# Two heads take turns on TensorE in two attentions; S5's inner product gets 32-column stationary sides in column groups

## The chip, the cores and the metric

The kernel runs on one core of a Trainium2 chip. The metric is the device time of one execution in microseconds (us), the median of several runs. TensorE (PE in the profile) multiplies a stationary operand, loaded by LDWEIGHTS (PEld), with a moving operand that streams through; VectorE is DVE, ScalarE ACT, GpSimd POOL, and SP issues most DMAs.

## The reference

Two model blocks run over 256 tokens of width 2048, one after the other. The parts that the change touches are, in short:

```python
# block 1, sparse attention (NSA): 16 heads of 64, 4 key groups; compressed, selected and window branches
s_c = einsum('bsgrd,bngd->bgrsn', q, kc) * scale + bias_c          # 15 compressed keys
s   = einsum('bqgrd,bqgkd->bgrqk', qc, ks) * scale + bias          # selected; the window branch has the same form
pr  = softmax(s);  o = einsum('bgrqk,bqgkd->bqgrd', pr, vs)
o   = gt[0] * o_c + gt[1] * o_s + gt[2] * o_w
# block 2, layer 0, gated linear attention (GLA): 8 heads, keys of 64
S_t = diag(a_t) S_{t-1} + k_t^T v_t;  o_t = q_t S_t
# block 2, layer 1, S5: 128 groups of 16 channels with 64 complex states, and a skip d
x_t = lam x_{t-1} + b u_t;  y_t = Re(C x_t) + d u_t
```

Around them stand large products with weights (w_in, w_out, MLP, feed forward, gates) in float32 accuracy.

## The kernel before, in words

**The large products.** `group` (L287 on) computes 512 output columns in four tiles of 128. Each weight chunk is loaded by SP, split by ACT (`wh`, L261) and DVE (`wl`, L262) into two fp32r parts, and multiplied by L304. All mixing work is put between these products: a generator (`self.mix`) is advanced one step per weight chunk by `mix_step`, and the S5 preparation (`s5_gen`, `self.bg`) a step or so per group by `bg_step`, at lower priority, so that the scheduler puts its products one by one between those of L304. The order on each engine is fixed when the program is built.

**f32 products.** The mixers multiply in plain f32. The trace records each such product as two MATMUL records (called passes here), each with a LDWEIGHTS of its own. A transpose is one record.

**NSA** (`nsa_gen`, L903 on). A tile t holds two heads, e = 0 on partitions 0 to 63 and e = 1 on 64 to 127. For each unit (t, c, e), c being the half of the 256 queries, `scores` makes two products (L957) of 64 rows by 128 columns into one `px` bank, and a softmax on DVE and ACT (L962 to L971); `turn` transposes (L980) and ACT copies (L982); `values` multiplies by the values (L996, 128 rows by 64 columns, output partitions by e), after L990 for a tile's first unit. One step of the generator does `values` of one unit, `turn` of the next and `scores` of the one after. `comp` (L922) makes the compressed branch's scores, four products of e = 0, then four of e = 1. `px` and `pm` have two banks each.

**GLA** (`gla_gen`, L1255 on). For each of eight levels, `decayed` scales queries and keys two levels ahead (DVE, ACT, POOL), and `scores(lv, e)` makes eight products (L1328, 64 rows by 128 columns; four at the last level, L1335) of one head half e, one e per step; DVE copies them under a mask (L1331). Before it, L1290 makes the diagonal, two banks of one e per step.

**S5's inner matrices** (`prod` and `toep` in `s5_gen`). For each of 16 k, eight products (L1691, stationary 128 by 128, moving 16 columns) give a matrix that ACT copies, POOL adds d to, TensorE transposes (L1699), and ACT copies again; a DMA writes it to DRAM in windows (`TTd`). `s5` later uses products with 32-column stationary sides side by side in four column groups (L1816).

Of the kernel before, what the change touches and what calls it, by code (L numbers as in the profile page):

```python
# [26 lines left out]
# columns of w_in  # L27
# [3 lines left out]
# ------------------------------------------------------------------ host side  # L31
# [26 lines left out]
def layout(inp):  # L58
    """Host side: transposes, reshapes, concatenation and constants of the shapes."""
# [15 lines left out]
    # block-diagonal LRU gates: tile t holds blocks 2t, 2t+1  # L75
# [32 lines left out]
    gm = np.zeros((P, 7, 64), np.uint32)       # gm[s, level, j]: s in the left half of the block of right position j  # L108
# [5 lines left out]
    gp = lambda a: np.ascontiguousarray(a.reshape(64, 2, 64).transpose(1, 2, 0).reshape(P, 64))   # [g, p] -> [(g2 p), pair]  # L114
# [8 lines left out]
    dd = np.zeros((16, 16, 8, 16), np.float32)                                                # [h, k, g, h']  # L123
    dd[np.arange(16), :, :, np.arange(16)] = g["s5_d_2"][0].reshape(16, 8, 16).transpose(2, 0, 1)
    o["s5d"] = dd.reshape(16, 16, P)
# [10 lines left out]
# ------------------------------------------------------------------ device side  # L136
class K:
    def __init__(self, tc, I, out, es, dump=None):
# [16 lines left out]
        self.hold = ()                # instructions the background work stays behind  # L155
# [9 lines left out]
    def bg_step(self, n=1):  # L165
        """emit the next pieces of the work that runs behind the products"""
# [23 lines left out]
    # tiles  # L190
# [62 lines left out]
    def wload(self, pieces, shape=(P, 2, 512)):  # L253
        """pieces: list of (index into tile, dram ap). Returns rounded and rest parts of the chunk."""
# [24 lines left out]
    def mix_until(self, made):  # L279
        """maker of tile k for a product whose operand comes from the mixer, which notes its tiles in made"""  # L280
# [59 lines left out]
    def evac(self, ps, out=None, mul=None, add=None):  # L340
        """out <- (product (+ add)) (* mul), the halves of a wide product added"""
# [26 lines left out]
    # norms  # L368
# [9 lines left out]
    def stat(self, acc, y, k):  # L378
        """acc += y^2 for tile k of 16; the last four stay apart, for TensorE to sum"""
# [8 lines left out]
    def rsqrt_small(self, v, n):  # L388
        """v [128,n] (positive) -> v**-0.5"""
# [14 lines left out]
    def bcast(self, r, dst):  # L404
        """r [128 tok, 2] -> dst [128, 256]: row of r on every partition"""
# [8 lines left out]
    def log_exp(self):  # L414
        """ScalarE's tables for Ln and Exp, after the activation noted last"""
# [10 lines left out]
    def rnorm(self, acc, n, dst, fill=0):  # L426
        """acc [128,256] partial sums of squares -> dst [128,256]: rsqrt(mean+eps) on every partition"""
# [16 lines left out]
        # one Newton step  # L444
# [5 lines left out]
    def rnorm_tok(self, acc, n):  # L450
        """the same with the token on the partition: [128 tok, 2]"""
# [17 lines left out]
    # ------------------------------------------------------------------ stages  # L469
# [30 lines left out]
    def make_x(self, gain):  # L500
        """X <- split(h*gain), a tile at a time: returns X and the maker of tile k"""
# [16 lines left out]
    def post_norm(self, Y, acc, fill=20):  # L518
        """maker of h's tile k: h += Y * rsqrt(mean y^2)   (Y is y times gain)"""
# [15 lines left out]
    def put_ys(self, Y, acc, k0, ys, gain):  # L535
        """Y[k] <- y*gain; acc += y^2"""
# [34 lines left out]
    def exp_small(self, x, n, alloc=None):  # L571
        """exp on [128,n] for -87 < x < 88, to float32 accuracy"""
# [22 lines left out]
    def bias_tables(self):  # L595
        """relative position bias: reversed table in DRAM, and the compressed branch's bias"""
# [12 lines left out]
        # compressed: bias[q, c, e, t, n], distance q + 128c - 16n - 31; the table's column for it is 159 - 128c + 16n,  # L609
        # and past its end every distance is negative  # L610
# [13 lines left out]
    def block1_in(self):  # L624
# [40 lines left out]
        # selected and window keys  # L665
# [9 lines left out]
        # selected and window values, token on the partition  # L675
# [12 lines left out]
        # gates  # L688
# [32 lines left out]
    def thin(self, Xk, wh, wl, n, mul, out=None):  # L721
        """T layout product with few columns, times mul: [n, 256]"""
# [11 lines left out]
    def amode(self, ps, X, c, wh, wl, first, last):  # L734
        """token layout product: ps [128 tok, n] += x[:, chunk c]^T w, w [128 k, n]"""
# [6 lines left out]
    def lru_open(self, UG):  # L742
        V = self.nc.vector
        # c4 = 2*softplus(-lam); halves of the biases
# [747 lines left out]
    def s5_gen(self):  # L1492
# [213 lines left out]
        for k in range(16):  # L1706
# [13 lines left out]
            if pend:  # L1720
                prod()
# [255 lines left out]
```

## Time and profile before

| what | value |
|---|---|
| median of 3 runs | 3699.75 us (3696.19 to 3700.69) |
| span of the profiled execution, first to last instruction | 3695.8 us |
| PE busy | 3534.8 us, 96% |
| DVE, ACT, POOL busy | 63%, 50%, 28% |
| NSA stretch, 206 to 444 us | PE busy 231.3 of 237.6 us |
| GLA stretch, 1405 to 1505 us | PE busy 100.0 of 100.0 us |
| mean granted TensorE clock | 0.981 |

The profiled execution's own time beside its span is not listed; the runs lie 0.4 to 4.9 us above the span. A record's duration on PE overlaps the next record's, so what a product costs is read from the distance between starts: how much later the products behind it start than at their usual pace.

### The profile page before, as it was taken

To read this page: it belongs to the slowest core of one execution; us is meant where nothing else is said; L and a number is where in the kernel's file an instruction comes from. 1 tells how busy PE (TensorE), PEld (TensorE's weight loads), DVE (VectorE), ACT (ScalarE), POOL (GpSimd) and SP (SyncE) were. 2 spreads that over 40 slices of the span, in tenths; PEclk is the share of its full clock that TensorE was granted. 3 is DMA by queue.
4 is the path that set the end of the run, shared out by engine and by line. 5 is a ranking of instruction groups with operands and counts; after the bars stand their busy time and mean duration, and the time that the engine had idled before them with its cause. 6 is when DMAs were issued, how large, how long until landed. Compare 5 with 4: busy or idle time off the path is not lost. (4 is left out here: it accounts for less than half of the span.)

```text
span 3695.8 us, 59166 instructions
## 1 busy us (share of the span) xinstructions
PE 3534.8 (96%) x22214; PEld 3113.5 (84%) x22214; DVE 2337.9 (63%) x3610; ACT 1836.0 (50%) x2895; POOL 1020.8 (28%) x1466
## 2 busy tenths in 40 slices
PE   8989989999999999999899999999779999999998
PEld 8878878888888898999887888888668888888887
DVE  6676596566656775455865466666765765565556
ACT  4655564544445653445544344444555554444444
POOL 1221122288730112011615555555410200000000
PEclk9999999999999999999999999999989999999999
DMA  8644345666776564565567777777776466565663
GB/s 214 204 117 139 115 144 190 187 199 204 231 219 195 175 201 123 143 177 181 164 197 218 224 215 229 235 220 258 251 228 186 145 189 187 185 191 188 188 188 128
DMA packets 506552, 699.61 MB, mean 189 GB/s; under 512 B 43239, under 2 KB 317671, under 8 KB 506264
## 3 DMA queue, kind: packets, MB, share of 16 engines
q1 hardware_dynamic: 472848, 628.60, 54.9%
q0 software_dynamic: 27120, 63.05, 5.9%
q10 hardware_dynamic: 6296, 4.17, 0.4%
q8 instruction: 174, 2.85, 0.3%
q14 instruction: 114, 0.93, 0.1%
HBM read 654.22 MB, written 37.22 MB: 187 GB/s over the span
## 5 line engine op out<-in xcount | busy, mean ns | idle before, releaser
L304 PE MATMUL ps<-x,wh 128*128 128x512 f32 (+1 forms) x8560 | 2503.9, 355 | 68.3 <-ACT wh L261 21.3
L262 DVE TENSOR_TENSOR wl<-wr,wh 128x1024 fp32r<-128x1024 f32 x1126 | 1432.1, 1277 | 1132.6 <-ACT wh L261 1123.3
L304 PE MATMUL ps<-x,wl 128*128 128x256 f32 x6832 | 1924.2, 283 | 1.3 <-DVE wl L262 1.3
L261 ACT ACTIVATE wh<-wr 128x1024 fp32r<-128x1024 f32 x1126 | 1184.7, 1057 | 1311.4 <-PE ps L304 1023.9
L304 PEld LDWEIGHTS ps<-x,wh 128*128 128x128 f32 x8560 | 1511.2, 191 | 321.8 <-ACT wh L261 22.9
L304 PEld LDWEIGHTS ps<-x,wl 128*128 128x128 f32 x6832 | 1305.5, 191 | 10.8 <-issue 3.5
L304 PE MATMUL px<-x,wh 128*128 128x512 f32 (+1 forms) x1776 | 660.1, 397 | 12.5 <-DVE x L249 7.0
L304 PE MATMUL px<-x,wl 128*128 128x256 f32 x1744 | 492.4, 282 | 1.2 <-DVE wl L262 1.2
L304 PEld LDWEIGHTS px<-x,wh 128*128 128x128 f32 x1776 | 333.8, 189 | 91.1 <-DVE x L249 8.5
L304 PEld LDWEIGHTS px<-x,wl 128*128 128x128 f32 x1744 | 331.6, 190 | 2.7 <-DVE wl L262 2.1
L527 POOL TENSOR_TENSOR e<-x,r_c 128x256 f32<-128x256 f32 x40 | 34.6, 871 | 1039.3 <-DVE r_c L448 1026.9
L1748 POOL TENSOR_TENSOR m<-m,m 128x256 f32<-128x256 f32 x64 | 64.5, 1020 | 326.8 <-PE pm L1691 236.8
L357 ACT ACTIVATE e<-ps 128x256 f32<-128x256 f32 x324 | 119.9, 376 | 67.6 <-PE ps L304 57.9
L376 POOL TENSOR_TENSOR acc<-acc,sq 128x256 f32<-128x256 f32 x89 | 79.6, 894 | 260.4 <-ACT sq L375 257.8
L245 ACT ACTIVATE x<-e 128x256 fp32r<-128x256 f32 x168 | 67.9, 410 | 88.6 <-DVE e L1473 42.8
L246 DVE TENSOR_TENSOR x<-e,x 128x256 fp32r<-128x256 f32 x168 | 78.0, 473 | 27.7 <-ACT x L245 25.1
L1731 POOL TENSOR_TENSOR m<-m,m 128x128 f32<-128x128 f32 x128 | 86.0, 694 | 10.7 <-DMA TTd<-m 10.7
L361 DVE TENSOR_TENSOR e<-ps,e 128x256 f32<-128x256 f32 x168 | 69.8, 416 | 6.3 <-ACT e L357 6.3
L1730 POOL TENSOR_TENSOR m<-m,m 128x128 f32<-128x128 f32 x128 | 70.1, 575 | 0.3
L1749 POOL TENSOR_TENSOR m<-m,m 128x256 f32<-128x256 f32 x64 | 64.1, 1002 | 5.3 <-DMA BBd<-m 1.8
L738 PE MATMUL ps<-wh,x 128*128 128x512 f32 x160 | 64.7, 405 | 0.0
L1750 POOL TENSOR_TENSOR m<-m,m 128x256 f32<-128x256 f32 x64 | 62.4, 974 | 2.1
(495 smaller groups left out, 2977.8 us busy)
## 6 DMA issues: line engine op xcount, KB each, us to landing
wr<-in_w_ffn_in_dram SPq DMA_DIRECT2D x704, 256.0 KB, 3.3
wr<-in_mlp_w_dram SPq DMA_DIRECT2D x256, 512.0 KB, 4.3
wr<-in_w_ffn_out_dram SPq DMA_DIRECT2D x176, 512.0 KB, 4.3
wr<-in_w_in_dram SPq DMA_DIRECT2D x152, 512.0 KB, 3.8
wr<-in_w_out_dram SPq DMA_DIRECT2D x64, 512.0 KB, 3.7
wr<-in_w_glu_dram SPq DMA_DIRECT2D x128, 256.0 KB, 3.2
wr<-in_ple_gate_dram SPq DMA_DIRECT2D x32, 512.0 KB, 4.5
wr<-in_w_in_dram SPq DMA_DIRECT2D x32, 256.0 KB, 5.4
```

The lines of the kernel that those rows point to most:

```text
L245: a = nc.scalar.activation(dst[:, 0], src, AF.Copy)
L246: b = (eng or nc.vector).tensor_tensor(dst[:, 1], src, dst[:, 0].bitcast(F32), op=ALU.subtract)
L261: nc.scalar.activation(wh, wr, AF.Copy)
L262: nc.vector.tensor_tensor(wl, wr, wh.bitcast(F32), op=ALU.subtract)
L304: mm = lambda o, w, x, a, z: nc.tensor.matmul(o, w, x, start=a, stop=z, skip_group_check=True)
L357: a = S.activation(t, ps[:, T:2 * T], AF.Copy)
L361: self.hold = a, V.tensor_tensor(y, ps[:, 0:T], t, op=ALU.add)
L376: (eng or nc.vector).tensor_tensor(acc, acc, q, op=ALU.add)
L738: nc.tensor.matmul(ps, xh, wh, start=first, stop=False, skip_group_check=True)
L1730: G_.tensor_tensor(cx[:, q], u_(0), l_(0), op=ALU.mult)
L1731: G_.tensor_tensor(t1[:, q], u_(1), l_(1), op=ALU.mult)
L1748: G_.tensor_tensor(ob[:, :, ri], v4(gb[0][:, 0]), v4(gb[1][:, ri]), op=ALU.mult)
```

## The change

In NSA the unit is now (t, c). `products` makes the score products of both heads, e = 0 and 1 in turn, into two `px` banks; `soft` does one head's softmax, one per step; the transposes of e = 0 and e = 1 come in the two following steps, and `values` takes both heads, in turn, another step later. `comp` alternates e as well. In GLA both e of a level are multiplied in one step, alternating, into two banks; the masked copies of e = 0 come in that step and those of e = 1 in the next. In S5 the operands of the inner product change sides: the stationary side is B for two groups of channels side by side with zeros in the other's place (32 columns), the moving side C (128 columns), the output a quarter of the partitions; two products add up in it. Its result needs no transpose, d comes as [128, 16], and one ACT copy, one PE transpose and one `pm` tile go per k.

```diff
 # nsa_gen
-            for e in range(2):
-                ps = self.ps("px")
-                for t in range(4):
-                    nc.tensor.matmul(ps[:, t * 16:t * 16 + 15], q[e * 64:e * 64 + 64, th * 4 + t, c * P:(c + 1) * P],
+            pss = [self.ps("px") for _ in range(2)]
+            for t in range(4):
+                for e in range(2):
+                    nc.tensor.matmul(pss[e][:, t * 16:t * 16 + 15], q[e * 64:e * 64 + 64, th * 4 + t, c * P:(c + 1) * P],
...
+        def products(u):
+            t, c = u
...
+            ps = [self.ps("px") for _ in range(2)]
+            for b in range(2):
+                for e in range(2):
+                    er = slice(e * 64, e * 64 + 64)
+                    nc.tensor.matmul(ps[e][:, b * T:b * T + nk], q[er, t, c * P:(c + 1) * P], ksw[b][er, t // 2, 0:nk],
+                                     start=True, stop=True)
+            return ps
+        def soft(u, e, ps):
...
-                nc.tensor.matmul(yp[e * 64:e * 64 + 64, c * P:(c + 1) * P], vv[b][:, kc, g * 64:g * 64 + 64], PT[:, i],
-                                 start=False, stop=(i == n - 1), skip_group_check=True)
+                for e in range(2):
+                    nc.tensor.matmul(yp[e * 64:e * 64 + 64, c * P:(c + 1) * P], vv[b][:, kc, g * 64:g * 64 + 64],
+                                     PT[e][:, i], start=False, stop=(i == n - 1), skip_group_check=True)
...
-            for u in [(t, c, e) for t in range(th * 4, th * 4 + 4) for c in range(2) for e in range(2)]:
+            for u in [(t, c) for t in range(th * 4, th * 4 + 4) for c in range(2)]:
                 if u2:
                     values(*u2)
-                u2 = (u1[0], turn(*u1)) if u1 else None
-                u1 = (u, scores(u))
+                PT = [turn(u1[0], u1[1][0])] if u1 else None
+                ps = products(u)
+                pr = [soft(u, 0, ps[0])]
+                yield 1
+                if u1:
+                    PT.append(turn(u1[0], u1[1][1]))
+                    u2 = u1[0], PT
+                pr.append(soft(u, 1, ps[1]))
+                u1 = u, pr
                 yield 1
 # gla_gen
-            for e in range(2):
-                yield 1
-                scores(lv, e)
+            yield 1
+            pss = scores(lv)
+            keep(lv, 0, pss[0])
+            yield 1
+            keep(lv, 1, pss[1])
 # s5_gen, prod and toep
-            for q in range(8):
-                nc.tensor.matmul(kt[:, q * 16:q * 16 + 16], cx[q // 4][:, q % 4].rearrange("p t h -> p (t h)"),
-                                 bb[:, q], start=True, stop=True)
-            S.activation(bt[:, 2], kt[:, 0:P], AF.Copy)
-            G_.tensor_tensor(bt[0:16, 2], bt[0:16, 2], bt[0:16, 3], op=ALU.add)
...
-            nc.tensor.transpose(pt[:, 0:P], bt[:, 2], self.ident)
+            for i in range(2):
+                for r in range(4):
+                    q = 2 * r + i
+                    nc.tensor.matmul(kt[r * 32:r * 32 + 32, 0:P], bt[:, i, r * 32:r * 32 + 32],
+                                     cx[q // 4][:, q % 4].rearrange("p t h -> p (t h)"), start=(i == 0), stop=(i == 1),
+                                     skip_group_check=True)
...
+            G_.tensor_tensor(kp[:, 112:128], kp[:, 112:128], bt[:, 2, 0:16], op=ALU.add)
...
-            G_.tensor_tensor(bb, cb[:, 1, 0], n_(0), op=ALU.mult)
-            G_.tensor_tensor(t1, cb[:, 1, 1], n_(1), op=ALU.mult)
-            G_.tensor_tensor(bb, bb, t1, op=ALU.add)
+            for w in range(2):
+                G_.tensor_tensor(cb[:, 1, w], cb[:, 1, w], n_(w), op=ALU.mult)
+            for i in range(2):
+                G_.tensor_tensor(bt[:, i].rearrange("p (r two) h -> p r two h", two=2, h=16)[:, :, i],
+                                 pairs(cb[:, 1, 0])[:, :, i], pairs(cb[:, 1, 1])[:, :, i], op=ALU.add)
```

On PE, in the first half of NSA, before the change (`pm` 2853 is the output of tile t = 2, `px` 2916 its scores):

```order
L304 MATMUL ps_2821<-x_86,wh_2933 128x256
L980 MATMUL pm_2797<-cst,m_2749 128x128
L990 MATMUL pm_2853<-x_721,VB 128x256
L980 MATMUL pm_2797<-cst,m_2749 128x128
L304 MATMUL ps_2821<-x_86,wh_2933 128x256
L304 MATMUL ps_2821<-x_86,wl_2934 128x256
L304 MATMUL ps_2822<-x_86,wh_2933 128x256 x2
L996 MATMUL pm_2853<-m_2800,x_721 64x128 x2
L957 MATMUL px_2916<-x_720,q 128x256 x2
L304 MATMUL ps_2822<-x_86,wl_2934 128x256
```

The same engine and half after the change (L999 is the former L990, L1006 L996, L988 L980, L960 L957):

```order
L304 MATMUL ps_2356<-x_87,wl_2692 128x256
L999 MATMUL pm_2719<-x_721,VB 128x256
L1006 MATMUL pm_2719<-m_2622,x_721 64x128
L1006 MATMUL pm_2719<-m_2675,x_721 64x128
L1006 MATMUL pm_2719<-m_2622,x_721 64x128
L1006 MATMUL pm_2719<-m_2675,x_721 64x128
L988 MATMUL pm_2725<-cst,m_2630 128x128 x4
L960 MATMUL px_2735<-x_720,q 128x128
L960 MATMUL px_2736<-x_720,q 128x128
L960 MATMUL px_2735<-x_720,q 128x128
L960 MATMUL px_2736<-x_720,q 128x128
L304 MATMUL ps_2355<-x_87,wh_2755 128x256 x2
```

Both heads' values and scores now stand in one piece at a chunk's boundary, alternating; 14 of the 16 score units stand like this, the other two (t = 0, c = 0 and t = 3, c = 1) still have L304's between their heads.

On PE, the first of S5's inner products (k = 0), before:

```order
L304 MATMUL px_10255<-x_9275,wl_10372 128x256
L1691 MATMUL pm_10232<-m_9318,m_9537 128x16
L304 MATMUL px_10256<-x_9275,wh_10371 128x512
L1691 MATMUL pm_10232<-m_9318,m_9537 128x16
L304 MATMUL px_10256<-x_9275,wl_10372 128x256
```

The same after (L1720 is the former L1691):

```order
L1720 MATMUL pm_10236<-m_9539,m_9318 32x128
L304 MATMUL px_10261<-x_9275,wh_10376 128x512
L1720 MATMUL pm_10236<-m_9539,m_9318 32x128
L304 MATMUL px_10261<-x_9275,wl_10377 128x256
L1720 MATMUL pm_10236<-m_9763,m_9318 32x128
L304 MATMUL ps_10262<-x_9275,wh_10376 128x512
```

The products stand where they stood: over all 16 k, before, 88 alone between L304's, eight fours and one eight; after, 88 alone, eight fours, a three and a five. The rest of the order on PE is as before, apart from the 16 transposes of L1699 that are gone.

## Rows read from the trace of the kernel before

**Rows 1.** Page, part 1: busy us (share of the span) xinstructions, by engine.
```profile
PE 3534.8 (96%) x22214; PEld 3113.5 (84%) x22214; DVE 2337.9 (63%) x3610; ACT 1836.0 (50%) x2895; POOL 1020.8 (28%) x1466
```

**Rows 2.** Windows NSA and GLA: length, busy us by engine (x instructions), clock, DMA.
```profile
206.40:444.00 237.60, 231.27 (x1620) 201.25 (x1619) 144.20 (x458) 124.74 (x281) 30.53 (x39) 0.97 0.39 121
1405.00:1505.00 100.00, 100.00 (x627) 86.06 (x626) 58.47 (x160) 38.54 (x45) 27.95 (x16) 1.00 0.40 116
```

**Rows 3.** Timeline, PE, two NSA score units: start us, us, engine, line, xpasses.
```profile
255.44 1.13 PE L957 MATMUL px<-x,q 64*128 64x256 f32 x4
...
265.32 0.28 PE L304 MATMUL ps<-x,wh 128*128 128x256 f32 x1
265.53 0.71 PE L957 MATMUL px<-x,q 64*128 64x128 f32 x4
266.17 0.39 PE L304 MATMUL ps<-x,wh 128*128 128x256 f32 x1
266.39 0.28 PE L304 MATMUL ps<-x,wl 128*128 128x256 f32 x1
```

**Rows 4.** Timeline, PE, values of one head at c = 1.
```profile
420.44 0.28 PE L304 MATMUL ps<-x,wh 128*128 128x256 f32 x1
420.70 1.09 PE L996 MATMUL pm<-m,x 128*64 128x128 f32 x8
421.72 0.39 PE L304 MATMUL ps<-x,wh 128*128 128x256 f32 x1
421.94 0.28 PE L304 MATMUL ps<-x,wl 128*128 128x256 f32 x1
422.06 0.40 PE L304 MATMUL ps<-x,wh 128*128 128x256 f32 x2
```

**Rows 5.** Timeline, PE, GLA's scores of one e at level 0.
```profile
1429.34 2.00 PE L1328 MATMUL px<-x 64*128 64x64 f32 x16
1431.26 0.50 PE L738 MATMUL ps<-wh,x 128*128 128x512 f32 x1
1431.60 0.39 PE L739 MATMUL ps<-wl,x 128*128 128x512 f32 x1
1431.83 0.40 PE L740 MATMUL ps<-wh,x 128*128 128x512 f32 x1
```

**Rows 6.** Timeline, PE: compressed scores of both e, of one, and S5's column groups.
```profile
206.59 1.53 PE L922 MATMUL px<-kcmp,q 64*128 64x15 f32 x16
...
328.63 1.06 PE L922 MATMUL px<-kcmp,q 64*128 64x15 f32 x8
...
2705.42 0.64 PE L1816 MATMUL px<-wh,x 128*32 128x128 f32 x16
```

**Rows 7.** Timeline, PE, one of S5's inner products between L304's.
```profile
974.53 0.28 PE L304 MATMUL px<-x,wl 128*128 128x256 f32 x1
974.64 0.29 PE L1691 MATMUL pm<-m,m 128*128 128x16 f32 x2
974.79 0.48 PE L304 MATMUL px<-x,wh 128*128 128x512 f32 x1
975.10 0.29 PE L1691 MATMUL pm<-m,m 128*128 128x16 f32 x2
```

**Rows 8.** Timeline, PE, a lone f32 product of a narrow tile between L304's.
```profile
56.91 0.28 PE L304 MATMUL ps<-x,wl 128*128 128x256 f32 x1
57.12 1.03 PE L603 MATMUL px<-oh,relb 33*16 33x511 f32 x2
58.07 0.50 PE L304 MATMUL ps<-x,wh 128*128 128x256 f32 x2
58.41 0.28 PE L304 MATMUL ps<-x,wl 128*128 128x256 f32 x1
```

**Rows 9.** Waits of PE in the NSA window: us in total, times, longest us.
```profile
PE pm L942 <- DVE m L936: 4.0, 1, 4.0
PE pm L980 <- DVE m L971: 2.0, 4, 1.3
```

More of the change, by code (lines that the diff above doesn't have):

```diff
@@ L945, in nsa_gen @@
         Bts, yps = {}, {}
-        def scores(u):
-            t, c, e = u
-            if c == 0 and e == 0:
+        def products(u):
+            t, c = u
+            if c == 0:
                 Bts[t] = Bt = self.m([P, 2, T])
-                for e_ in range(2):
-                    nc.gpsimd.dma_start(Bt[:, e_], tab[2 * t + e_])
-            Bt, nk, off, hh = Bts[t], P * (c + 1), P * (1 - c), 2 * t + e
-            er = slice(e * 64, e * 64 + 64)
-            ps = self.ps("px")
-            for b in range(2):
-                nc.tensor.matmul(ps[:, b * T:b * T + nk], q[er, t, c * P:(c + 1) * P], ksw[b][er, t // 2, 0:nk],
-                                 start=True, stop=True)
+                for e in range(2):
+                    nc.gpsimd.dma_start(Bt[:, e], tab[2 * t + e])
+            nk = P * (c + 1)
+            ps = [self.ps("px") for _ in range(2)]
[6 more added lines that the diff above has]
+        def soft(u, e, ps):
+            t, c = u
+            Bt, nk, off, hh = Bts[t], P * (c + 1), P * (1 - c), 2 * t + e
             pr = self.m([P, 2, T])
@@ L985, in values @@
         def values(u, PT):
-            t, c, e = u
+            t, c = u
             g, r2 = t // 2, (t % 2) * 64
-            if c == 0 and e == 0:
+            if c == 0:
                 yps[t] = self.ps("pm")
@@ L995, in values @@
                 b, kc = i // (c + 1), i % (c + 1)
-                nc.tensor.matmul(yp[e * 64:e * 64 + 64, c * P:(c + 1) * P], vv[b][:, kc, g * 64:g * 64 + 64], PT[:, i],
-                                 start=False, stop=(i == n - 1), skip_group_check=True)
-            if c == 1 and e == 1:
+                for e in range(2):
+                    nc.tensor.matmul(yp[e * 64:e * 64 + 64, c * P:(c + 1) * P], vv[b][:, kc, g * 64:g * 64 + 64],
+                                     PT[e][:, i], start=False, stop=(i == n - 1), skip_group_check=True)
+            if c == 1:
                 y = yp[:, 0:T]
@@ L1284, in gla_gen @@
         EQ = [yv[:, 3072:4096].rearrange("p (i t) -> p i t", i=4), gl[:, 12:16]]
-        for e in range(2):
-            er = slice(e * 64, e * 64 + 64)
-            for b in range(2):
-                ps = self.ps()
-                for i in range(4):
-                    nc.tensor.matmul(ps[:, i * P:(i + 1) * P], gk[er, i, b * P:(b + 1) * P], gq[er, i, b * P:(b + 1) * P],
-                                     start=True, stop=True)
-                V.tensor_tensor(ST[:, e, b], ps.rearrange("p (i t) -> p i t", i=4),
+        for b in range(2):
+            pss = [self.ps() for _ in range(2)]
+            for i in range(4):
+                for e in range(2):
+                    er = slice(e * 64, e * 64 + 64)
+                    nc.tensor.matmul(pss[e][:, i * P:(i + 1) * P], gk[er, i, b * P:(b + 1) * P],
+                                     gq[er, i, b * P:(b + 1) * P], start=True, stop=True)
+            for e in range(2):
+                V.tensor_tensor(ST[:, e, b], pss[e].rearrange("p (i t) -> p i t", i=4),
                                 self.ident[:, None, :].to_broadcast([P, 4, P]), op=ALU.mult)
@@ L1316, in decayed, with scores, keep @@
             G.tensor_tensor(eb[:, :, 0], blk(gk)[:, :, 0], eb[:, :, 0], op=ALU.mult)
-        def scores(lv, e):
+        def scores(lv):
             half = 1 << lv
             qk = EQ[lv % 2]
-            er = slice(e * 64, e * 64 + 64)
-            ps = self.ps()
-            if lv < 7:
-                for b in range(2):
-                    for i in range(4):
-                        right = qk[er, i, b * P:(b + 1) * P].rearrange("p (n two h) -> p n two h", two=2, h=half)[:, :, 1]
-                        o = (b * 4 + i) * 64
-                        nc.tensor.matmul(ps[:, o:o + 64], qk[er, i, b * P:(b + 1) * P], right, start=True, stop=True)
+            pss = [self.ps() for _ in range(2)]
+            for m in range(8 if lv < 7 else 4):
+                b, i = m // 4, m % 4
+                for e in range(2):
+                    er = slice(e * 64, e * 64 + 64)
+                    if lv < 7:
+                        right = qk[er, i, b * P:(b + 1) * P].rearrange("p (n two h) -> p n two h", two=2, h=half)[:, :, 1]
+                        o, left = pss[e][:, m * 64:m * 64 + 64], qk[er, i, b * P:(b + 1) * P]
+                    else:
+                        o, left, right = pss[e][:, i * P:(i + 1) * P], qk[er, i, 0:P], qk[er, i, P:T]
+                    nc.tensor.matmul(o, left, right, start=True, stop=True)
+            return pss
+        def keep(lv, e, ps):
+            half = 1 << lv
+            if lv < 7:
                 dst = ST[:, e].rearrange("p b i t -> p (b i) t").rearrange("p m (n two h) -> p m n two h", two=2, h=half)
@@ L1333, in scores @@
             else:
-                for i in range(4):
-                    nc.tensor.matmul(ps[:, i * P:(i + 1) * P], qk[er, i, 0:P], qk[er, i, P:T], start=True, stop=True)
                 S.activation(ST2[:, e], ps.rearrange("p (i t) -> p i t", i=4), AF.Copy)
@@ L1342, in gla_gen @@
                 decayed(lv + 1)
-            for e in range(2):
-                yield 1
-                scores(lv, e)
+            yield 1
[3 more added lines that the diff above has]
+            keep(lv, 1, pss[1])
         while "vr" not in self.ready:
@@ L1708, in s5_gen @@
             cb, ll = self.m([P, 2, 2, 8, 16]), self.m([P, 2, 8, 8])
-            bt = self.m([P, 4, P])
+            bt = self.m([P, 3, P])
+            G_.memset(bt[:, 0:2], 0.0)
             src = I["s5cb"][k]
@@ L1712, in s5_gen @@
             G_.dma_start(ll, LD[:, :, kg:kg + 8])
-            G_.dma_start(bt[0:16, 3], I["s5d"][:, k])
-            bb, t1 = bt[:, 0].rearrange("p (g h) -> p g h", g=8), bt[:, 1].rearrange("p (g h) -> p g h", g=8)
+            G_.dma_start(bt[:, 2, 0:16], I["s5d"][:, k])
             n_ = lambda w: self.rp[:, w, kg:kg + 8].unsqueeze(2).to_broadcast([P, 8, 16])
-            G_.tensor_tensor(bb, cb[:, 1, 0], n_(0), op=ALU.mult)
-            G_.tensor_tensor(t1, cb[:, 1, 1], n_(1), op=ALU.mult)
-            G_.tensor_tensor(bb, bb, t1, op=ALU.add)
+            pairs = lambda a: a.rearrange("p (r two) h -> p r two h", two=2)
+            for w in range(2):
+                G_.tensor_tensor(cb[:, 1, w], cb[:, 1, w], n_(w), op=ALU.mult)
+            for i in range(2):
+                G_.tensor_tensor(bt[:, i].rearrange("p (r two h) -> p r two h", two=2, h=16)[:, :, i],
+                                 pairs(cb[:, 1, 0])[:, :, i], pairs(cb[:, 1, 1])[:, :, i], op=ALU.add)
             yield 1
             if pend:
-                prod()
+                kp = prod()
             cxs = []
@@ L1754, in s5_gen @@
                 yield 1
-                prod()
+                kp = prod()
                 yield 1
-                toep()
+                toep(kp)
                 pend = None
```

22 lines of the change are left out of this document (11 added, 11 removed).

## The prediction

> **What bounds the kernel now.** I read the page's busy shares first, then the windows of the stretches that the change touches, then PE's timeline inside them, and the waits last. PE is busy for 96% of the span [rows 1], and in the stretches themselves for 231.3 of 237.6 us (NSA) and 100.0 of 100.0 us (GLA), while DVE is busy for 144.2 and 58.5 us of them and ACT for 124.7 and 38.5 [rows 2]. So time that goes on PE there is time that goes from the span, as long as the softmax and the weight splitting keep up; they have room for about a third more work in the same time.
>
> Busy time on PE says little of what a product costs, since records overlap. The reader is to look at distances between starts. L304's narrow products start every 0.12 us (421.94 to 422.06) [rows 4]. Two passes of a score product of 64 rows are put in between: from 265.32 to 266.39 pass 1.07 us, of which two L304's usual 0.24, so the four passes of a unit at c = 0 cost 0.83 [rows 3]. Passes of 128 columns follow each other every 0.11 (the eight of rows 4 take 1.09 against a first one of some 0.3), so 4 x 0.11 = 0.44 are passes and 0.39 is the price of going in and out: the next L304 comes 0.64 after the first pass instead of 0.44, the one behind it 0.22 later instead of 0.12, and the first pass 0.21 after the last L304 [rows 3]. A block costs 0.39 plus its passes. At c = 1 the four passes last 0.42 longer (1.13 against 0.71), so a unit costs 1.25 [rows 3]. Eight passes of values: 420.44 to 421.94 less 0.24 is 1.26; four, then, 1.26 - 0.44 = 0.82 [rows 4]. Sixteen passes of GLA: 1429.34 to 1431.60 less one L738 of 0.23 (1431.60 to 1431.83), plus 0.09 on the way in as in rows 3, is 2.12 [rows 5].
>
> Do two halves of the array run beside each other? Compressed scores of one head half (8 passes) last 1.06, of e = 0 and then e = 1 in one block (16) 1.53 and not 1.06 + 0.88 = 1.94 [rows 6]: the second half's rows started while the first's passes were still queued. And 16 passes in four column groups last 0.64 [rows 6] where 16 in one group last 2.00 [rows 5]. So both row groups and column groups overlap here; alternated, two equal streams should take the time of one.
>
> **The change part by part.**
>
> Scores of NSA. Now 16 units at 0.83 and 16 at 1.25: 33.3 us. After: by the order 14 pairs stand together and cost one unit each, 7 x 0.83 + 7 x 1.25 = 14.6, and two pairs stay apart (2 x 0.83 + 2 x 1.25 = 4.2): 18.8. Gain 14.5.
>
> Values. Now 16 x 0.82 + 16 x 1.26 = 33.3; after, half of it, since the two heads' outputs lie in different column groups, and column groups run beside each other in S5's products [rows 6]. Gain 16.6. The Trainium skill, "TensorE: Matmul & The Clock Gate", section "The mechanism", speaks against it: by it a weight load overlaps a running product only where the row group differs, which column groups do not. By that rule two column streams would follow each other, and the gain would be 6.2 (rival 2); the 16 passes in 0.64 us [rows 6] do not agree with it.
>
> Compressed scores. Now four blocks of 8 passes (0.39 + 0.88 = 1.27) and two of 16, 0.47 longer (1.53 - 1.06): 1.74; together 8.6. After, four blocks of 16 passes in two streams, 1.27 each: 5.1. Gain 3.5.
>
> Waits in NSA. PE waits 4.0 us for L936 and 2.0 for L971 [rows 9]. The first belongs to the compressed softmax, whose DVE work is the same: it stays. The second goes, since a transposition comes two steps after its scores instead of one. Gain 2. What is late next: `products` takes both `px` banks, and the one of e = 1 is read by DVE only a step (some 24 L304's, 2.9 us) before it is wanted again. The reads stand at the head of that step's DVE work, so I cost this at nothing; if DVE were late, L304 behind it would wait and with it everything (the third rival). The softmax results and their transposes are held longer in the nine 2 KB tiles; four are taken per unit and are free again by the next unit but one: nothing.
>
> GLA. Now 14 blocks of 2.12, two of 16 passes on the diagonal, some 2.15 each, and two of 8 at the last level, 1.27: 36.5. After, 7 x 2.12, two blocks of 8 beside 8 (1.27) and one of 4 products beside 4 (1.27): 18.7. Gain 17.8. Behind it DVE has 16 masked copies per level instead of two times 8, the same work; `decayed` still has its three steps until its scores. Cost nothing; cover: DVE's 58 of 100 us become 58 of 82.
>
> S5. Here the products stay one by one between L304's. Now one costs 0.23: from 974.64 to 975.10 pass 0.46, of which one wide L304 0.23 [rows 7]. 88 of these are 20.2, eight fours at no more than 4 x 0.23 and an eight make some 9, and 16 transposes of a pass each 1.8: 31. After, each has a tile of 32 columns. The trace has one product of this kind alone between L304's: 56.91 to 58.41 is 1.50, less three L304's 0.36 is 1.14, less its two passes of 511 columns leaves 0.28 for going in and out [rows 8]: 128 more columns cost a pass 0.105 (rows 3, 0.42 over four passes), so one of 511 takes 0.11 + 3 x 0.105 = 0.43. I take 0.30. With two passes of 128 columns: 0.30 + 0.22 = 0.52. 98 blocks (88 alone, ten groups, whose column groups overlap) make 98 x 0.52 = 51. Loss 20. Bounds: as now, 0.23, if the way in and out cost nothing more (then 22.5 and a gain of 8), and 0.61, if it cost the 0.39 of rows 3 (60, a loss of 29). I take 0.52, the row with the nearest shape.
>
> The rest of S5 is off PE: POOL has one memset and one small addition more and one product less per k, ACT one copy less; POOL is at 28% [rows 1], and nothing on PE waits for it there. The skip's DMA has 128 short rows instead of 16 long ones, 16 times, on POOL's queue behind the same loads: nothing.
>
> Sum: 14.5 + 16.6 + 3.5 + 2 + 17.8 = 54.4 gained, 20 lost: 34. The span of 3695.8 becomes 3661.5; the runs' median lies 4 us above the span, so 3699.75 - 34 = 3665.5, call it 3665.
>
> **The rivals.**
>
> 1. S5's products cost what they cost now. For it: they are surrounded by L304's today too and pay 0.23. Against it: today's tile is the whole array like L304's, and the lone narrow product pays more [rows 8]. Gain 8 instead of loss 20: 3637.
>
> 2. Column groups do not gain from alternating. The overlap part of the values' gain is lost and only the ways in and out are saved, 16 x 0.39 = 6.2 instead of 16.6: 3676. For it: a weight load of one group has to pass the other group's running product, and the trace has no two alternating column groups of 64. Against it: four groups of 32 take 0.64 us for 16 passes [rows 6]. It is what the page named at the values would give.
>
> 3. NSA becomes bound by something else. Its 238 us shrink to about 201 and DVE's 144 stay: 72%, with each softmax a chain through DVE, ACT and DVE and only two `px` banks. If half of NSA's 36.6 comes back as waits: 3683.
>
> 4. Slower than before: each of a lone S5 product's two passes pays the way in and out by itself, because the second pass's weights cannot be loaded while the array changes its tile. Price 2 x 0.52 = 1.04 per product, 102 us instead of 31, a loss of 71 against 54: 3716. It decides from 85 / 98 = 0.87 us per product. Against it: in rows 8 both passes together paid 0.3.
>
> 5. The change does not do what it says: alternated row and column groups run one after the other, since each product's two passes hold up the next. Then only the ways in and out go: 14 for scores, 16 for values and 8 for GLA at 0.39 are 15 us, with the waits 17, against 20: 3703. Against it: rows 6, as far as they show a block of one half behind a block of the other.
>
> **How the numbers follow.** The forecast 0.60, with a range of its own of 3652 to 3678 (S5 at 0.61 and at 0.40); rival 1 0.10, rival 2 0.08, rival 3 0.11, rival 4 0.07, rival 5 0.04. The range 3636 to 3686 takes in the forecast and rivals 1 to 3. A difference of 0.2% (7.4 us) is about what a measurement can tell from none: faster than that are the forecast and rivals 1 to 3, 0.89; within it rival 5, 0.04; slower rival 4, 0.07.
>
> **What would show it.** In the profile of the changed kernel: L960's eight passes in about the 0.71 and 1.13 us that four take now; L1006's 16 in about 1.1; L1350's 32 in about 2.0, and GLA's stretch some 18 us shorter. Between L304's, L1720's two passes with starts 0.5 us further apart than L304's pace, and S5's stretches longer by about 20 us in all. Wrong would be: L304's of NSA with waits on DVE or ACT beyond the 6 us of now; a pair in two times 0.71; L1720 at 0.23 or beyond 0.87.

## The result, and the profile after

| | median us | lowest to highest |
|---|---|---|
| before | 3699.26 | 3696.19 to 3700.69 |
| after | 3661.01 | 3654.79 to 3666.71 |

The ratio is 0.9896 (95% interval 0.9876 to 0.9916): 38 us faster, forecast 34. The span went from 3695.8 to 3655.6 us, 40.2 less. By first starts of the same lines, NSA with what follows it up to the first L424 took 33.8 us less (236.4 instead of 270.2), GLA 18.0 less (113.5 instead of 131.4), and the two stretches with S5's products 7.7 more (436.9 instead of 429.2) and 4.4 more (951.7 instead of 947.2); the rest is under 2 us a piece.

Page, part 1, and the windows of NSA and GLA, which answer to [rows 1, 2]:

```profile
PE 3501.3 (96%) x22198; PEld 3060.9 (84%) x22198; DVE 2353.4 (64%) x3610; ACT 1833.1 (50%) x2879; POOL 1022.5 (28%) x1498
```

```profile
206.40:410.30 203.90, 195.80 (x1599) 176.96 (x1599) 142.91 (x463) 124.40 (x285) 29.75 (x41) 0.96 0.45 139
1377.40:1459.40 82.00, 82.00 (x628) 70.72 (x627) 59.90 (x160) 38.52 (x45) 27.02 (x16) 1.00 0.49 141
```

DVE and ACT do in the shorter stretches what they did in the longer ones: DVE 142.91 us where it had 144.20, now 70% of the time. Softmax and masked copies kept up.

The timeline of PE (start us, us, engine, line, shapes, passes): compressed scores of both heads, values of both at c = 1, a pair of scores at c = 0 and one at c = 1 [rows 3, 4, 6]:

```profile
206.56 1.07 PE L922 MATMUL px<-kcmp,q 64*128 64x15 f32 x16
...
246.43 1.09 PE L1006 MATMUL pm<-m,x 128*64 128x128 f32 x16
...
256.85 0.72 PE L960 MATMUL px<-x,q 64*128 64x128 f32 x8
...
265.26 1.13 PE L960 MATMUL px<-x,q 64*128 64x256 f32 x8
```

Eight passes of scores take the 0.71 and 1.13 us that four took, sixteen of values the 1.09 of eight; compressed scores fall from 1.53 to 1.07. Of GLA's level the reader sees the two streams themselves:

```profile
1399.81 0.32 PE L1350 MATMUL px<-x 64*128 64x64 f32 x1
1399.98 0.27 PE L1350 MATMUL px<-x 64*128 64x64 f32 x1
1399.98 0.27 PE L1350 MATMUL pm<-x 64*128 64x64 f32 x1
1400.09 0.27 PE L1350 MATMUL px<-x 64*128 64x64 f32 x1
...
1401.75 0.50 PE L738 MATMUL ps<-wh,x 128*128 128x512 f32 x1
```

`px` and `pm`, the two heads, start within 0.01 us of each other, and behind the first pair one comes every 0.11 us. The whole level lasts from 1399.81 to 1401.75, 1.94 us: 32 passes in the time that 16 took, 1429.34 to 1431.26 [rows 5].

S5's lone product [rows 7]:

```profile
1035.70 0.50 PE L304 MATMUL px<-x,wh 128*128 128x512 f32 x1
1036.13 0.41 PE L1720 MATMUL pm<-m,m 128*32 128x128 f32 x2
1036.47 0.38 PE L304 MATMUL px<-x,wl 128*128 128x256 f32 x1
1036.78 0.41 PE L1720 MATMUL pm<-m,m 128*32 128x128 f32 x2
```

From 1036.13 to 1036.78 pass 0.65 us, of which a narrow L304 is 0.12: 0.53 where it was 0.23.

Waits of PE in the NSA window [rows 9]:

```profile
PE pm L943 <- DVE m L937: 4.5, 1, 4.5
PE px L436 <- POOL acc L376: 2.3, 1, 2.3
...
PE pm L988 <- DVE m L979: 0.3, 1, 0.3
```

The compressed softmax still stops PE (4.5), the transposes nearly no more (0.3 instead of 2.0), and there is a new wait: L436, which sums squares for a norm of another part, comes 17.5 us earlier than before (293.0 instead of 310.5) and now waits 2.3 us for POOL's additions. Behind this wait the granted clock was 0.50 (1.2 GHz) from 293.8 to 304.0 us, and four score passes of 256 columns took 1.95 us instead of 1.13:

```profile
293.63 1.95 PE L960 MATMUL px<-x,q 64*128 64x256 f32 x4
```

### The profile page after: what moved, and what is told of

Same layout as the page of the kernel before. It is cut to its first block, busy times and chain, and to the rows that moved or that the text cites. A ratio compares the mean times of both kernels' runs of the same rounds, so it can differ in the third digit from the quotient of the medians.

```text
span 3655.6 us, 59158 instructions
## 1 busy us (share of the span) xinstructions
PE 3501.3 (96%) x22198; PEld 3060.9 (84%) x22198; DVE 2353.4 (64%) x3610; ACT 1833.1 (50%) x2879; POOL 1022.5 (28%) x1498
## 5 line engine op out<-in xcount | busy, mean ns | idle before, releaser
L304 PE MATMUL ps<-x,wh 128*128 128x512 f32 (+1 forms) x8560 | 2498.4, 355 | 62.1 <-DVE e L361 19.3
L304 PE MATMUL ps<-x,wl 128*128 128x256 f32 x6832 | 1922.4, 283 | 0.8 <-DVE wl L262 0.8
L304 PEld LDWEIGHTS ps<-x,wh 128*128 128x128 f32 x8560 | 1510.7, 191 | 319.5 <-issue 30.3
L304 PEld LDWEIGHTS ps<-x,wl 128*128 128x128 f32 x6832 | 1306.1, 191 | 11.1 <-issue 5.6
L304 PE MATMUL px<-x,wh 128*128 128x512 f32 (+1 forms) x1776 | 658.3, 396 | 11.2 <-DVE x L249 6.8
L304 PE MATMUL px<-x,wl 128*128 128x256 f32 x1744 | 491.7, 282 | 0.5 <-DVE wl L262 0.5
L304 PEld LDWEIGHTS px<-x,wh 128*128 128x128 f32 x1776 | 332.6, 189 | 94.4 <-DVE x L249 8.6
L304 PEld LDWEIGHTS px<-x,wl 128*128 128x128 f32 x1744 | 330.5, 190 | 4.8 <-issue 3.2
L246 DVE TENSOR_TENSOR x<-e,x 128x256 fp32r<-128x256 f32 x168 | 86.0, 521 | 26.4 <-ACT x L245 22.6
L1779 POOL TENSOR_TENSOR m<-m,m 128x256 f32<-128x256 f32 x64 | 59.6, 932 | 71.7 <-DMA m<-in_s5bT_dram 71.0
L1780 POOL TENSOR_TENSOR m<-m,m 128x256 f32<-128x256 f32 x64 | 73.7, 1152 | 0.1
L738 PE MATMUL ps<-wh,x 128*128 128x512 f32 x160 | 64.6, 404 | 0.0
L740 PE MATMUL ps<-wh,x 128*128 128x512 f32 x160 | 63.2, 395 | 0.0
```

The lines of the kernel that those rows point to most:

```text
L246: b = (eng or nc.vector).tensor_tensor(dst[:, 1], src, dst[:, 0].bitcast(F32), op=ALU.subtract)
L304: mm = lambda o, w, x, a, z: nc.tensor.matmul(o, w, x, start=a, stop=z, skip_group_check=True)
L738: nc.tensor.matmul(ps, xh, wh, start=first, stop=False, skip_group_check=True)
L1780: G_.tensor_tensor(t1, v4(gb[0][:, 1]), v4(gb[1][:, 1 - ri]), op=ALU.mult)
```

## The experiments

All were timed beside the kernel before; its median was 3689 to 3699 in these sets, so kernels of different sets are compared by their ratios to it. A "price by starts" is summed over all pieces of a line: how much later the products behind a piece start than at L304's usual pace.

**Attentions alone (e1_attn) and S5 alone (e2_s5).** The layout of d and `s5_gen` from `prod` on are exchanged between the two kernels; e1_attn, against the changed kernel:

```diff
-                    nc.tensor.matmul(kt[r * 32:r * 32 + 32, 0:P], bt[:, i, r * 32:r * 32 + 32],
-                                     cx[q // 4][:, q % 4].rearrange("p t h -> p (t h)"), start=(i == 0), stop=(i == 1),
+                nc.tensor.matmul(kt[:, q * 16:q * 16 + 16], cx[q // 4][:, q % 4].rearrange("p t h -> p (t h)"),
+                                 bb[:, q], start=True, stop=True)
```

> The changed kernel with S5's inner product as it was before (stationary 128 by 128, moving 16 columns, one transpose per k); both attentions alternate. By starts on TensorE, the S5 products of the changed kernel cost 54.3 us (98 blocks) and those of before 33.5 (with the transposes). Theory A, each lone product with a 32-column tile costs the program its 0.53 us instead of 0.23: 3661 - 20.7 = 3640. Rival B, part of that time is taken out of waits that stand in the same stretch (from the first S5 product to the S5 layer's first rows the changed kernel lost only 7.7 + 4.4 = 12.1 us): 3649. Rival C, the S5 part costs nothing in all: 3661.

> The kernel before with the S5 part of the change alone. Theory A (0.53 us instead of 0.23 for a lone product, and the transposes gone): 3699 + 20.7 = 3720. Rival B (part of it comes out of waits of the same stretch): 3699 + 12 = 3711. Rival C (S5 costs nothing): 3699. In the profile the lone products of L1720's form should again cost 0.53 by starts.

Measured: attentions alone 3636.27, ratio 0.9853 (0.9832 to 0.9875): a gain of 54 us. S5 alone 3716.91, ratio 1.0073 (1.0051 to 1.0094): a loss of 27. By starts S5's products cost 32.0 (e1_attn, with the transposes) and 54.6 us (e2_s5, 98 places). C is out. The changed kernel once more, beside the same runs of before, is to tell A from B:

> The changed kernel once more, beside the runs of the kernel before on the chip of these experiments, so that it is compared with the others there. Ratio to before as in the first measurement, 0.9896 (0.9876 to 0.9916). With before at 3689 as in the first four experiments that is 3651; the S5 part would then have cost 15 (attentions alone, 3636) to 28 us (S5 alone, 3717 against 3689), the 20 of the forecast between them.

3654.51, ratio 0.9887 (0.9864 to 0.9911). From e1_attn's 0.9853 to the two ratios of the changed kernel it is 13 to 16 us, from before to e2_s5 27; A's 21 lies between, B's 12 is not excluded.

**One after the other in a piece (e4_serial), and longer turns (e5_turns).** The loops over e go outside the products, or half outside:

```diff
-            for m in range(8 if lv < 7 else 4):
-                b, i = m // 4, m % 4
-                for e in range(2):
+            for e in range(2):                      # e4; scores, values, comp and the diagonal alike
+                for m in range(8 if lv < 7 else 4):
+                    b, i = m // 4, m % 4
```

> The changed kernel, with the same products in the same pieces, but in a piece first all of e = 0, then all of e = 1 (scores, values, compressed scores of NSA, all of GLA's scores). Theory A, only taking turns lets two halves of the array run beside each other: a piece grows by half its passes at 0.11 (0.21 where they have 256 columns): scores 7 x 0.44 + 7 x 0.86 = 9.1, values 8 x 0.44 + 8 x 0.88 = 10.6, compressed scores 4 x 0.47 = 1.9, GLA 7 x 1.76 + 2 x 0.88 + 0.88 = 15: 36.6 in all, 3698. Rival E, a piece of one half behind a piece of the other overlaps too, as the compressed scores did in the kernel before (16 passes in 1.53 us instead of 1.94): a half of that, 3679. Rival F, the gain was the ways in and out alone: 3661, unchanged.

> The changed kernel with longer turns: scores, values, compressed scores and GLA's diagonal change the head every two products (four passes), GLA's levels every four products (eight passes). Theory G, which the pieces of one half behind the other suggest (scores, 4 passes behind 4: 1.36 against 1.29 us, nothing lost; values, 8 behind 8: 1.77 against 1.28; GLA, 16 behind 16: 3.67 against 2.13): the passes of one half run beside the last three or four of the other. Then turns of four passes cost what turns of two do (values at c = 1 1.28, compressed scores 1.19, diagonal 1.29 a piece), and GLA's levels, with three changes, lie at 2.8 to 3.2 us: 7 us slower than the changed kernel. Rival H, only turns of a single product overlap: values 1.77, compressed scores 1.66, diagonal 1.84, GLA 3.67: 17 us slower.

e4_serial: 3672.27, ratio 0.9958 (0.9941 to 0.9975), against 0.9896 and 0.9887: some 25 us lost. By starts a level of GLA costs 3.67 us instead of 2.13, values of both heads at c = 1 1.77 instead of 1.28, compressed scores 1.66 instead of 1.19; pairs of scores lose next to nothing. All pieces together lose 18 us. A's 37 and F's nothing are both wrong, E's half is close, and the timeline of PE shows why:

```profile
1407.47 1.66 PE L1350 MATMUL px<-x 64*128 64x64 f32 x13
1408.87 0.32 PE L1350 MATMUL pm<-x 64*128 64x64 f32 x1
1408.97 0.27 PE L1350 MATMUL px<-x 64*128 64x64 f32 x1
1409.03 0.27 PE L1350 MATMUL pm<-x 64*128 64x64 f32 x1
1409.09 0.27 PE L1350 MATMUL px<-x 64*128 64x64 f32 x1
1409.14 0.27 PE L1350 MATMUL pm<-x 64*128 64x64 f32 x1
1409.20 0.27 PE L1350 MATMUL px<-x 64*128 64x64 f32 x1
1409.25 1.65 PE L1350 MATMUL pm<-x 64*128 64x64 f32 x13
```

Thirteen passes of e = 0 run alone, its last three beside the first three of e = 1, and thirteen of e = 1 alone. The other half starts when three passes of the first are left. e5_turns, with changes every four or eight passes: 3660.06, ratio 0.9905 (0.988 to 0.993); values 1.33, compressed scores 1.21, diagonal 1.39, GLA's levels 2.74. That is G, with GLA's levels just under its 2.8 to 3.2: turns of four passes are nearly as good as turns of one product, and the two further changes in GLA save 0.93 us (3.67 to 2.74), some four passes each. H is out.

**S5's products in one piece (e3_block).** All eight get the same priority:

```diff
+            p0 = self.tc.cur_priority
             for i in range(2):
                 for r in range(4):
                     q = 2 * r + i
                     nc.tensor.matmul(kt[r * 32:r * 32 + 32, 0:P], bt[:, i, r * 32:r * 32 + 32],
...
+                    self.tc.cur_priority = p0
```

> The changed kernel, with the eight S5 products of a k given one priority, so that most stand in one piece (10 pieces of eight, 5 of seven with a lone one) instead of one by one. Theory A, the price of a lone product is the way in and out of the tile, paid once per piece, and four column groups run beside each other: a piece at 0.65 to 0.9 us, 16 of them some 12 us and five lone ones 2.7, instead of 54.3: 40 us less, 3621; if the waits of the stretch give part of it back as between before and after (12.1 of 20.7 showed), 3638. Rival D, the price belongs to each product, by its two passes of 128 columns and its own weights: a piece costs 0.3 + 16 x 0.11 = 2.1, 16 pieces 33 us: 3640 to 3645, and in the profile a piece lasts over 1.7 us.

3599.16, ratio 0.9754 (0.9732 to 0.9776): 90 us faster than before and some 50 faster than the changed kernel, the best version here. A piece on PE's timeline:

```profile
1859.26 0.28 PE L304 MATMUL ps<-x,wl 128*128 128x256 f32 x1
1859.46 0.64 PE L1721 MATMUL pm<-m,m 128*32 128x128 f32 x16
1860.04 0.50 PE L304 MATMUL ps<-x,wh 128*128 128x512 f32 x1
1860.38 0.28 PE L304 MATMUL ps<-x,wl 128*128 128x256 f32 x1
```

Sixteen passes last 0.64 and cost 0.77 us with the way in and out; all pieces together 16.7 instead of 54.3. D is out. The time won 13 us more than these 37.6, which the next runs are about.

**The whole width, and half of it (e6_full, e10_w64).** The stationary side is taken 128 or 64 columns wide, with output ranges side by side and four ACT copies per k instead of one:

```diff
-                    nc.tensor.matmul(kt[r * 32:r * 32 + 32, 0:P], bt[:, i, r * 32:r * 32 + 32],
+                    nc.tensor.matmul(kt[:, r * P:r * P + P], bt[:, i],     # e10: 64 rows of kt, 64 columns of bt
```

> The changed kernel with S5's products on the whole width of the array: stationary 128 by 128, moving 128 columns, into four ranges of a bank, of which four ACT copies take a quarter of the rows each; the products stand one by one as in the changed kernel. Theory A, the 0.53 us of a lone product are two passes and the way into a 32-column tile and out of it: without the tile 0.23 to 0.25, 98 places cost 25 instead of 54 us, 25 to 29 us faster than the changed kernel. Rival D, the 128 moving columns are the price: 0.5 again, no change.

> The changed kernel with 64-column stationary sides in S5's products (two ranges of a bank for each half of the partitions, four ACT copies), one by one. Theory A, the price is the way into a tile narrower than the array and out of it, whatever its width: between the 0.53 of 32 columns and the 0.39 + 0.22 = 0.61 that NSA's values of 64 columns suggest, 3655 to 3663. Rival P, the price goes with the columns that are left out: halfway between 0.53 and 0.226, 0.38: 3640.

e6_full (with its start flags some of the products do not enter the sum, a relative error of 0.039; all of them run): 3614.69, ratio 0.9789 (0.9754 to 0.9823). e10_w64: 3661.26, ratio 0.9896 (0.9877 to 0.9915). PE's timeline of the one and of the other:

```profile
937.32 0.39 PE L1720 MATMUL pm<-m,m 128*128 128x128 f32 x2
937.46 0.37 PE L304 MATMUL px<-x,wl 128*128 128x256 f32 x1
937.66 0.38 PE L1720 MATMUL pm<-m,m 128*128 128x128 f32 x2
```

```profile
1040.46 0.43 PE L1721 MATMUL pm<-m,m 128*64 128x128 f32 x2
1040.82 0.39 PE L304 MATMUL px<-x,wl 128*128 128x256 f32 x1
1041.14 0.43 PE L1721 MATMUL pm<-m,m 128*64 128x128 f32 x2
```

0.34 less 0.12 is 0.22 on the whole width, though 128 columns move; 0.68 less 0.12 is 0.56 with 64 columns (0.56 in the median too, 0.53 with 32). So these f32 products pay 0.31 to 0.34 for a tile narrower than the array, with 32 and with 64 columns alike. A holds for the price, D and P are out. The Trainium skill, "TensorEngine Tiling (Array Packing)", section "Key Properties", says that changing the tiling mode, not just the tile, drains the engine; these numbers agree, though no row shows which products it counts as a change of mode.

Narrowness alone is not the price. The kernel's fp32r products with few columns pay none: L728 has 16 columns, and in the changed kernel it starts 0.12 us behind L304, goes on every 0.11 to 0.12, and L738 behind it starts 0.11 later and L739 0.23 after that, their usual pace.

```profile
1367.66 0.28 PE L304 MATMUL ps<-x,wl 128*128 128x256 f32 x1
1367.78 0.39 PE L728 MATMUL ps<-x,wh 128*16 128x256 f32 x2
...
1373.11 0.28 PE L728 MATMUL ps<-x,wl 128*16 128x256 f32 x1
1373.22 0.40 PE L738 MATMUL ps<-wh,x 128*128 128x512 f32 x1
```

The same holds for L728 with 48 columns and L870 with 60. So the price is shown for plain f32 products; why the fp32r ones go without it is not shown.

But e6_full's products cost 31.9 us by starts, e1_attn's 32.0 with the transposes, and e6_full is faster by 0.0064 of the time, 24 us, or some 9 to 39 by the two intervals. Hence three runs on what stands behind the products.

**What the transposes cost (e7_oldblock, e8_noturn, e11_queue).** All three have the new attentions and the old products: in one piece by the edit of e3_block; without the first copy and the transpose (so with another matrix); and with the two early loads of the matrix from DRAM issued by GpSimd:

```diff
-            S.activation(bt[:, 2], kt[:, 0:P], AF.Copy)                                       # e8
-            nc.tensor.transpose(pt[:, 0:P], bt[:, 2], self.ident)
-            S.activation(kp[:, 112:240], pt[:, 0:P], AF.Copy)
+            S.activation(kp[:, 112:240], kt[:, 0:P], AF.Copy)
...
-                nc.sync.dma_start(tl[:, i], tt_src(len(tts)))
+                (nc.gpsimd if n == 2 else nc.sync).dma_start(tl[:, i], tt_src(len(tts)))     # e11
```

> Both attentions changed, S5's inner product as before the change (stationary 128 by 128, moving 16 columns), but its eight products of a k in one piece. Theory A, a product that has the whole array pays no way in and out, so a piece costs what eight lone ones do (16 passes at 0.11, 1.8 us a k): as with the products one by one, 3636. Rival J, which would explain why the 32-column products in one piece won more (52 us against the changed kernel, by medians of two chips) than their pieces got cheaper (54.3 to 16.7, 37.6 us): products put one by one between L304's cost the program more than their own time, by waits: 10 to 15 us faster, 3623.

> Both attentions changed, S5's products as before the change (128 by 128, 16 moving columns, one by one), but without what came behind them: the copy to a tile, d's addition in it, the transpose on TensorE and the second copy go; ACT copies the product once. The matrix is left untransposed, so the later part of S5 works on other values. Its products cost TensorE what those of the full-width form cost (0.226 us by starts in both), which ran 3615 where before ran 3699 (ratio 0.979); the form with the transposes ran at 0.984 to 0.985. Theory K, the two copies and the transpose behind POOL's addition hold up ACT's queue, and that is the difference: 3615 to 3622, and the stretch from 1630 us to the S5 layer's rows 915 to 922 us long instead of 938 to 943. Rival M, the difference lies elsewhere (the runs' scatter or the weights' transfers): 3638 to 3645, the stretch 937 or more.

> Both attentions changed, S5's inner product as before with its transposes, but the two early loads of its matrix (ttq from TTd, L1897), which stand in SP's queue ahead of weight loads, are issued by GpSimd. In the form with the transposes SP stood at these loads for 31.9 us (two times, up to 18.5), with 9.1 where the transposes were left out, 4.9 in the changed kernel; behind them ACT waited for w_ffn_out's chunks (40.6 us in all, up to 11.5) and TensorE for ACT (4.8). Theory Q, the wait in SP's queue is what the transposes cost beside their own time: ratio 0.979 to 0.981, some 3623, the feed forward's stretch 923 us instead of 938. Rival R, it is ACT's second copy or TensorE's order: 0.984 to 0.985, some 3640, the stretch 937 or more.

The stretch that is compared here is the feed forward's, in the changed kernel from the first L1421 to the first L1823. e7_oldblock: 3637.68, ratio 0.9838 (0.9813 to 0.9864), by the ratios 6 us less than e1_attn, but with a stretch of 942.5 us against 938.1; J's 10 to 15 us are not borne out, though the interval still reaches them. e8_noturn: 3623.32, ratio 0.9797 (0.9777 to 0.9816), its stretch 922.6 us long: K's size holds. K's place, ACT's queue behind the copies, is not what the rows point to; SP's and ACT's timelines of the kernel before:

```profile
2015.42 0.37 SPq L1870 DMA_DIRECT2D ttq<-TTd  x1
2015.88 12.19 SPq L258 DMA_DIRECT2D wr<-in_w_ffn_out_dram  x7
...
2021.13 1.06 ACT L261 ACTIVATE wh<-wr 128x1024 fp32r<-128x1024 f32 x1 [12.28 <-DMA wr<-in_w_ffn_out_dram]
```

and in SP's waits there and in the changed kernel (us in total, times, longest):

```profile
SPq L1870 <- DMA TTd<-m: 32.4, 2, 18.9
```

```profile
SPq L1901 <- DMA TTd<-m: 4.9, 2, 3.5
```

SP stands at a load of S5's matrix until the matrix has been written to DRAM, weight loads stand behind it, and ACT waits 12.28 us for weights. Without the transposes the matrix is written sooner: SP stands 9.1 us at its load in e8_noturn, 31.9 in e1_attn. e11_queue takes only this wait away: SP no longer stands there, ACT's waits for w_ffn_out fall from 40.6 to 13.2 us, TensorE's for ACT's `wh` from 5.2 to none, and the stretch is 928.6 us long; 3634.35, ratio 0.9822 (0.9798 to 0.9845). That is between Q's and R's, and its interval touches both. By these profiles the queue explains some 9 of the 15 us of the stretch, but two profiles of the changed kernel differ by 6 there (951.7 and 945.8). So it is shown that the wait goes with the queue, not how much of the time it explains; the rest stays open.

**A later copy (e9_late).** `kp`'s memset and copy move from `prod` to `toep`:

```diff
-            S.activation(kp[:, 112:240], kt[:, 0:P], AF.Copy)
-            return kp
+            return kt
...
+            S.activation(kp[:, 112:240], kt[:, 0:P], AF.Copy)
             G_.tensor_tensor(kp[:, 112:128], kp[:, 112:128], bt[:, 2, 0:16], op=ALU.add)
```

> The changed kernel with ACT's copy of an S5 product bank put some steps later, behind the next operands' work, so that the eight lone products are through when ACT comes to it. In the changed kernel ACT stands at this copy for 33.0 us in all in the stretch of the feed forward (11 times, up to 4.9), and TensorE waits there 16.7 us for banks that DVE frees (L361), against 3.8 in the full-width form. Theory L, the lone narrow products cost, beside their 0.3 us, what ACT's queue loses behind them: 8 to 15 us faster than the changed kernel, 3640 to 3647, and ACT's wait at the copy under 5 us. Rival N, the bank that is held longer is missed by others, or the waits come from elsewhere: 3655 or slower.

3672.54, ratio 0.9931 (0.9914 to 0.9947): slower, N. ACT no longer waits at the copy, but the matrix is written later, and the same queue gives the time back. SP's waits, and ACT's and PE's timelines:

```profile
SPq L1901 <- DMA TTd<-m: 33.2, 2, 21.3
```

```profile
1971.35 1.06 ACT L261 ACTIVATE wh<-wr 128x1024 fp32r<-128x1024 f32 x1 [18.14 <-DMA wr<-in_w_ffn_out_dram]
...
1974.85 0.79 PE L304 MATMUL ps<-x,wh 128*128 128x512 f32 x1 [16.02 <-DVE e L361]
```

ACT stands at the split of a late weight chunk, its copies of finished banks stand behind it, and PE waits 16.02 us for a bank. So L was not tested by itself: one edit changed two waits.

## Why the prediction was right, point by point

**The attentions.** Sum of the forecast 54.4; alone they gained 54 (46 to 62). NSA: 36.6 forecast, 33.8 seen. By starts scores gained 11.7 (14.5 forecast), values 21.4 (16.6), compressed scores 3.6 (3.5), transposes 2.9 (2): 39.6. A piece's way in is shared with its neighbour (values, transposes and scores now often stand together), so the single terms are less sure than their sum. Most of what the scores lack is the clock: behind the waits at L943 and L436 three of their pieces with 256 columns ran at a granted clock of 0.50, each some 1.2 us dearer, where before it was one, behind L942; the stretch has 17.0 us at that clock instead of 13.6. Of the 5.8 us between 39.6 and 33.8, L436's wait took 2.3, the mechanism of the third rival in small, but at POOL's sum of squares and not at the softmax, and the compressed softmax 0.5; some 3 stay open. GLA: 17.8 forecast, 18.0 seen. The rivals 2 and 5 are out by L1006's 16 passes in 1.09 us and L1350's 32 in 1.94. That alternating matters, and not only the common piece, is shown by e4_serial.

**S5.** The step "0.30 + 0.22 = 0.52" was right to 0.01, and its mechanism, for f32 products, is shown by e6_full, e10_w64 and e3_block. In place of 31 against 51 us stand 33.5 against 54.3. Rivals 1 and 4 are out. But one sign was missed: the two stretches with S5's products were to grow by about 20 us and grew by 12.1.

**What failed in it** is "The rest of S5 is off PE" with "nothing on PE waits for it there", a term put at nothing. By way of SP's queue, weights and ACT, PE does wait for the end of S5's chain: 5.2 us for `wh` in e1_attn, none in e11_queue, 16.02 in one place in e9_late. Taking the transposes away was worth 15 to 24 us (0.9853 and 0.9838 against 0.9797 and 0.9789), where their passes on PE are some 1.8; how much of that is the queue stays open, as said above. And the narrow tile cost more than its price by starts: from the changed kernel to e6_full it is 36 to 40 us by the ratios, of which 22.4 by starts. In the feed forward's stretch ACT stands at the copy behind the eight products for longer, and PE waits for banks; the changed kernel, then e6_full:

```profile
ACT m L1725 <- PE pm L1720: 33.0, 11, 4.9
...
PE ps L304 <- DVE e L361: 11.8, 6, 2.9
PE ps L304 <- DVE x L361: 4.9, 4, 2.0
```

```profile
ACT m L1726 <- PE pm L1720: 18.0, 10, 2.7
...
PE ps L304 <- DVE e L361: 2.3, 3, 1.2
PE ps L304 <- DVE x L361: 1.5, 1, 1.5
```

16.7 us of waits for banks (13.4 in the changed kernel's second profile) against 3.8 make up most of the difference; that ACT's place in its queue causes them is argued from these rows, not shown by a run of its own. e10_w64 fits, with 36.5 us at its copies and 15.6 at the banks; e1_attn does less, with 16.6 at the copy and 8.1 at the banks. The two terms that were missing, by these ratios some 18 gained and some 16 lost, nearly cancel: the net loss of 20 was right partly by luck.

## What to carry to other kernels

Count the ways in and out of a tile, not only the passes: an f32 product in a narrow tile between full-width ones paid 0.3 us each time, and eight of them in one piece, in four column groups, 0.77 together instead of eight times 0.53; the fp32r products of 16 to 60 columns paid nothing. Let two halves of the array take turns every few products; one long stream behind another overlapped here by three or four passes only. And follow the result of background work to its reader: if the load of it stands in a queue ahead of weights, its lateness is paid there.

## What the runs showed of the hardware that was not expected

- A lone f32 product cost the same with 16 and with 128 moving columns, 0.22 us, as long as its tile was the whole array; with a tile of 64 or 32 columns and 128 moving ones 0.56 and 0.53. An fp32r product of 16, 48 or 60 columns kept L304's pace.
- With the halves one after the other, the second started when three passes of the first were left in row groups (GLA in e4_serial). Column groups do much the same by their price: values, eight passes behind eight, cost 1.77 us, where 0.39 + 16 x 0.11 = 2.15 would be no overlap.
